# Fill weights of the banded attention: each load but the first placed behind the mask additions of the block whose scores were made last

## The chip, the cores and the metric

The kernel runs on one core of a Trainium2 chip. The metric is the device time of one execution, in microseconds (us). Three runs of the kernel before gave 1305.97, 1306.15 and 1306.93 us; the median is 1306.15 us. A core has a matrix engine (PE, whose weight loads are listed apart as PEld), a vector engine (DVE), an activation engine (ACT), a further engine (POOL) and an engine that here only issues transfers (SP). Each engine carries out its own instructions in a fixed order, which is settled when the kernel is built, and waits on semaphores for the others.

## What is computed

One decoder layer on a sequence of 1024 rows of width 1024: a token mixer, cross-attention, a gated MLP with a short convolution, and a final norm. The change touches the token mixer only. It projects the normalised input once and splits the result over two head groups, a gated linear attention (GLA) and a sliding-window softmax attention in banded blocks of 128 queries. Cut to what matters:

```python
hn = rms_norm(h, norm_mix[l])
proj = hn @ w_in[l]
gq, gk, gv, gr, ga, sq, sk, sv = jnp.split(proj, split_at, axis=-1)
o_gla = gla_mixer(gq, gk, gv, gr, ga, w_alpha[l], b_alpha[l], gla_gain[l])
o_swa = swa_mixer(sq, sk, sv, rel_bias, sinks[l])
h = h + jnp.concatenate([o_gla, o_swa], axis=-1) @ w_out[l]

def swa_mixer(q, k, v, rel_bias, sinks):          # per block of 128 queries, 256 keys
    s = jnp.einsum('bnqhgd,bnkhd->bnhgqk', qb, kk)
    s = jnp.where(mask, s + bias, -jnp.inf)
    m = jnp.maximum(jnp.max(s, axis=-1, keepdims=True), sink)
    p = jnp.exp(s - m)
    p = p / (jnp.sum(p, axis=-1, keepdims=True) + jnp.exp(sink - m))
    o = jnp.einsum('bnhgqk,bnkhd->bnqhgd', p, vv)
```

## The kernel before

Products of 32-bit numbers are made of three products of parts: every operand is split into a high part (ACT, a cast, L110) and a low part (DVE, the difference, L111), and `mm3` (L149, L150, L151) multiplies high by high, high by low and low by high. So the first two products of a weight tile need only its high part, the third its low part.

A weight tile of 1024 by 128 of `w_in` is made ready in four steps, all in `load`: a transfer of 512 KB into one of three staging tiles `st` (`fetch`, issued by SP), a multiplication by the norm's gains in place (DVE, L123), the cast into the high part `w` (ACT, L110), and the difference into the low part `w` (DVE, L111). There are six `w` tiles, that is three pairs.

The stage that the change touches is the banded attention, `swa`. It works on eight blocks, b = 0 to 7. Ahead of the loop the scores of block 0 are made. Then in pass b

1. `swa_softmax(b + 1)`: sixteen score products on PE (L1008) into four banks `psS`, then on DVE eight mask additions with a row maximum (L1017, each two instructions: the addition and the reading of the maximum), small operations on the row factors (`nm`, `es`, `den`), eight exponentials on ACT (L1026), and eight multiplications by the row factors on DVE (L1034); pass 7 has no such step, since there is no block 8;
2. the first half of a column tile of the GLA projection, 24 products on PE into a bank `psF` (`next(fill)`), evicted by DVE at L609;
3. `swa_transposed(b)`: transposes of block b's probabilities on PE, copied by ACT;
4. the second half of the same column tile, 24 products;
5. `swa_values(b)`: the products with the values on PE (L1061), whose result is split (ACT L110, DVE L111 into `pts`) and stored.

PE's order is written out by hand over this loop. It is the code's order. The GLA column tiles are the filling: eight of them, `gk` twice, `gq` twice, `gr` four times, made by the generator in `cols_gla`, one in each pass. Pass b uses column tile b. In pass 3 the fill also has transposes of the decayed keys (L711) ahead of its products, with copies on ACT (L712).

The orders of DVE, ACT and SP are not written out by hand here: when the kernel is built, a scheduler places their instructions. Nothing kept it from placing the preparation of the fill weights well ahead of their use. The call `issue_after(x)`, used elsewhere in the kernel already, tells it that the instructions made in its block that run on the same engine as x must stand behind x in that engine's order.

Of the kernel before, what the change touches and what calls it, by code (L numbers as in the profile page):

```python
# [24 lines left out]
ALU = mybir.AluOpType  # L25
# [3 lines left out]
P = 128  # L29
# [3 lines left out]
NK = D // P  # L33
# [10 lines left out]
NEG = -1e30  # L44
# [17 lines left out]
class Layer:  # L62
# [550 lines left out]
    def cols_gla(self, keep):  # L613


        w = self.a["w_in"][0]
        self.gk, self.gq, self.gr = [], [], []
        first = [self.load_cols(w, 256, self.mix_gains(0, NK))]

        def parts():  # L620
            for tiles, tag, c0, n, scale in ((self.gk, "gk", 256, 2, 1.0), (self.gq, "gq", 0, 2, 0.125),
                                             (self.gr, "gr", 1024, 4, 1.0)):
                for t in range(n):
                    dst = keep(tag, bufs=n)
                    tiles.append(dst)
                    weights = first.pop() if first else self.load_cols(w, c0 + P * t, self.mix_gains(0, NK))
                    yield from self.cols_parts(dst, weights, scale)
        return parts()

# [367 lines left out]
    def swa_softmax(self, b, new):  # L997

        nc = self.nc
        q = slice(b * P, (b + 1) * P)  # L1000
        k0, nk = self.swa_keys(b)
        off = 256 - nk
        ps = [[self.bank("S").rearrange("p (t k) -> p t k", t=2) for _ in range(2)] for _ in range(2)]
        for u in range(2):
            for t in range(2):
                for g in range(2):
                    pr = slice(64 * g, 64 * g + 64)
                    nc.tensor.matmul(ps[u][g][:, t, :nk], lhsT=self.sq[2 * u + t][pr, q], rhs=self.sk[pr, k0:k0 + nk],  # L1008
                                     start=True, stop=True)
        probs = []  # L1010
        for u in range(2):
            prob = new("prob", [P, 4, 256], bufs=4)
            mx = self.small("mx", [P, 4])
            for g in range(2):
                for t in range(2):
                    n = 2 * g + t
                    nc.vector.tensor_tensor_reduce(out=prob[:, n, :nk], in0=ps[u][g][:, t, :nk],  # L1017
                                                   in1=self.bias[g][:, 2 * u + t, off:], scale=1.0, scalar=NEG,
                                                   op0=ALU.add, op1=ALU.max, accum_out=mx[:, n:n + 1])
            nm = self.small("nm", [P, 4])  # L1020
            us = slice(4 * u, 4 * u + 4)
            nc.vector.scalar_tensor_tensor(out=nm, in0=mx, scalar=-1.0, in1=self.nsink[:, us], op0=ALU.mult,
                                           op1=ALU.min)
            den = self.small("den", [P, 4])
            for n in range(4):
                last = nc.scalar.activation(out=prob[:, n, :nk], in_=prob[:, n, :nk], func=AF.Exp,  # L1026
                                            bias=nm[:, n:n + 1], accum_out=den[:, n:n + 1])
            es = self.small("es", [P, 4])
            nc.vector.tensor_tensor(out=es, in0=nm, in1=self.sink[:, us], op=ALU.add)
            last = nc.scalar.activation(out=es, in_=es, func=AF.Exp)  # L1030
            nc.vector.tensor_tensor(out=den, in0=den, in1=es, op=ALU.add)
            nc.vector.reciprocal(out=den, in_=den)
            for n in range(4):
                nc.vector.tensor_scalar(out=prob[:, n, :nk], in0=prob[:, n, :nk], scalar1=den[:, n:n + 1],  # L1034
                                        scalar2=None, op0=ALU.mult)
            probs.append(prob)
        return probs, last
# [977 lines left out]
```

## Time and profile before

| what | us |
|---|---|
| median of three runs | 1306.15 |
| the profiled execution, its own time | 1307.37 |
| its span | 1305.5 |
| PE busy, 0 to 100 us | 94.42 |
| PE busy, 100 to 220 us | 119.42 |
| DVE busy, 100 to 220 us | 86.67 |
| ACT busy, 100 to 220 us | 64.47 |
| PE busy, 220 to 600 us | 379.82 |
| PE busy, 600 us to the end | 697.74 |

The span is what the trace covers; the execution's own time has 1.9 us more around it. The stretch from 100 to 220 us holds nearly the whole loop over the blocks. Rows of the timeline give the start and the length in us, then engine, line, operation, what it writes and reads, and in brackets the idle time ahead of it with what ended it. Products of PE overlap: the spacing of their starts is their price, not their length.

### The profile page before, as it was taken

Reading aid. Unit: us, or ns where it says so; the run is one execution under the profiler, and the core shown is the slowest. Engines: PE = TensorE matmul, PEld = TensorE weight load, DVE = VectorE, ACT = ScalarE, POOL = GpSimd, SP = SyncE. Lnnn points to the kernel's source line nnn. Section 1 sums busy time; section 2 is a strip of 40 time slices with the busy share of each in tenths; the row PEclk is TensorE's granted clock in tenths of the full one; section 3 lists DMA queues with packets and bytes.
Section 4 is the critical chain, followed back from the end, with each engine's and each line's share of the span. In section 5 each row is a group of like instructions: output and inputs, shape, how many; then the busy total and the mean of one; then the engine's idle time right before and its main releaser. Section 6 shows DMA issues by size and latency. Waiting matters only on the chain.

```text
span 1305.5 us, 17288 instructions
## 1 busy us (share of the span) xinstructions
PE 1291.4 (99%) x6539; PEld 1073.8 (82%) x6539; DVE 948.3 (73%) x1630; ACT 610.0 (47%) x1087; POOL 99.1 (8%) x173
## 2 busy tenths in 40 slices
PE   8999999999999999999999999999999999999997
PEld 8887777989888888888888888888888888888886
DVE  6848764368544333599689988888888886999687
ACT  5525545346433333565556544443444444454455
POOL 1400111101122000001100000000000000000001
PEclk9999999999999999999999999999999999999999
DMA  7642211239844311106422342232223138710204
GB/s 223 186 117 65 62 57 61 65 124 296 224 148 158 117 56 59 33 33 202 122 65 81 113 130 98 80 97 86 76 81 97 66 109 318 282 65 9 73 17 153
DMA packets 140056, 146.89 MB, mean 113 GB/s; under 512 B 15825, under 2 KB 108166, under 8 KB 139974
## 3 DMA queue, kind: packets, MB, share of 16 engines
q1 hardware_dynamic: 127670, 106.82, 26.6%
q0 software_dynamic: 12144, 38.71, 8.4%
q8 instruction: 51, 0.84, 0.3%
q10 hardware_dynamic: 160, 0.27, 0.1%
q14 instruction: 31, 0.25, 0.1%
HBM read 109.06 MB, written 38.28 MB: 113 GB/s over the span
## 4 chain that ended last, share of the span: by engine, by line
PE 96%; DVE 2%; DMA 1%; ACT 0%; issue 0%; SPq 0%; DVEq 0%; ACTq 0%
PE psS L1592 15%; PE psF L1592 13%; PE psF L149 10%; PE psF L150 10%; PE psF L151 10%; PE psS L1707 5%; PE psF L1707 5%; PE psS L1369 3%; PE psS L149 2%; PE psS L151 2%; PE psS L150 2%; PE psO L1707 2%; PE psT L1707 2%; PE psO L149 2%; PE psO L150 2%; PE psO L151 2%
## 5 line engine op out<-in xcount | busy, mean ns | idle before, releaser
L110 ACT CAST w<-st 128x1024 fp32r<-128x1024 f32 (+1 forms) x144 | 124.4, 866 | 251.9 <-PE psF L150 70.9
L111 DVE TENSOR_TENSOR w<-st,w 128x1024 fp32r<-128x1024 f32 (+1 forms) x144 | 142.4, 991 | 76.3 <-ACT w L110 75.6
L1621 DVE SCALAR_TENSOR_TENSOR uy<-uy,vec,uy 128x1023 f32<-128x1023 f32 (+1 forms) x88 | 112.1, 1279 | 1.9 <-ACT uy L1619 1.5
L1707 PE MATMUL psF<-w,w 128*128 128x512 f32 x318 | 89.3, 389 | 0.5 <-DVE w L111 0.5
L1707 PE MATMUL psS<-w,w 128*128 128x512 f32 x318 | 89.0, 389 | 0.0
L1592 PE MATMUL psS<-a,w 128*128 128x512 f32 x360 | 86.5, 389 | 0.0
L149 PE MATMUL psF<-xh,w 128*128 128x512 f32 x208 | 83.0, 399 | 0.0
L151 PE MATMUL psF<-xh,w 128*128 128x512 f32 x208 | 81.5, 392 | 0.0
L150 PE MATMUL psF<-xl,w 128*128 128x512 f32 x208 | 81.2, 390 | 0.0
L1592 PEld LDWEIGHTS psS<-a,w 128*128 128x128 f32 x360 | 67.6, 188 | 14.0
L1592 PE MATMUL psF<-a,w 128*128 128x512 f32 x324 | 77.8, 389 | 0.0
L1592 PEld LDWEIGHTS psF<-a,w 128*128 128x128 f32 x324 | 60.8, 188 | 12.6
L1707 PEld LDWEIGHTS psF<-w,w 128*128 128x128 f32 x318 | 59.6, 188 | 13.2 <-DVE w L111 0.9
L1707 PEld LDWEIGHTS psS<-w,w 128*128 128x128 f32 x318 | 59.7, 188 | 12.4
L1619 ACT ACTIVATE uy<-uy,vec 128x1024 f32<-128x1024 f32 x44 | 54.7, 1246 | 18.6 <-DVE uy L1612 18.3
L149 PE MATMUL psF<-act,w 128*128 128x512 f32 x160 | 63.2, 395 | 0.0
L150 PE MATMUL psF<-act,w 128*128 128x512 f32 x160 | 62.8, 392 | 0.0
L151 PE MATMUL psF<-act,w 128*128 128x512 f32 x160 | 62.5, 391 | 0.0
L1592 PE MATMUL psS<-act,wx 128*128 128x512 f32 x240 | 57.7, 389 | 0.0
L1592 PE MATMUL psS<-act,w 128*128 128x512 f32 x240 | 57.7, 389 | 0.0
L1592 PEld LDWEIGHTS psS<-act,wx 128*128 128x128 f32 x240 | 45.0, 188 | 9.4
L1592 PEld LDWEIGHTS psS<-act,w 128*128 128x128 f32 x240 | 45.0, 188 | 9.3
(464 smaller groups left out, 3082.6 us busy)
## 6 DMA issues: line engine op xcount, KB each, us to landing
st<-in_w_up_dram SPq DMA_DIRECT2D x44, 512.0 KB, 4.0
g_d<-uy POOLq DMA_DIRECT2D x22, 512.0 KB, 2.9
act<-in_w_down_dram SPq DMA_DIRECT2D x12, 512.0 KB, 9.1
st<-g_d SPq DMA_DIRECT2D x10, 512.0 KB, 3.9
res<-g_d SPq DMA_DIRECT2D x10, 512.0 KB, 9.1
st<-in_w_in_dram SPq DMA_DIRECT2D x9, 512.0 KB, 6.6
xt_d<-pts POOLq DMA_DIRECT2D x16, 256.0 KB, 4.6
ow_d<-pts POOLq DMA_DIRECT2D x32, 128.0 KB, 3.2
```

The source lines that it names most:

```text
L110: h = nc.scalar.copy(out=hi, in_=src)
L111: l = nc.vector.tensor_tensor(out=lo, in0=src, in1=hi.bitcast(F32), op=ALU.subtract)
L149: mm(out, lhsT=lh, rhs=rh, start=start, stop=False)
L150: mm(out, lhsT=lh, rhs=rl, start=False, stop=False)
L151: mm(out, lhsT=ll, rhs=rh, start=False, stop=stop)
L1369: mm(ps, lhsT=left[n][l][:, q], rhs=right[n][q][r], start=new and q == 0 and i == 0, stop=new and q == 3 and i == 2, skip_group_check=not new)
L1592: nc.tensor.matmul(ps, lhsT=b[l][:, q], rhs=a[q][r], start=first and q == 0 and n == 0, stop=first and q == 3 and n == 2, skip_group_check ...
L1619: nc.scalar.activation(out=y, in_=u, func=AF.Identity, scale=self.v("cw2", j), bias=self.v("conv_b", j))
L1621: nc.vector.scalar_tensor_tensor(out=y[:, s:], in0=u[:, :T - s], scalar=self.v(nm, j), in1=y[:, s:], op0=ALU.mult, op1=ALU.add)
L1707: nc.tensor.matmul(ps[i], lhsT=g[:, l, tk], rhs=w[:, r], start=first and k == 0 and m == 0, stop=first and k == n - 1 and m == 2, skip_gro ...
```

## The change

The last mask addition of each block is kept as `self.masked`, and the load of each fill weight but the first runs within `issue_after` of it.

```diff
                 for t in range(n):
                     dst = keep(tag, bufs=n)
                     tiles.append(dst)
-                    weights = first.pop() if first else self.load_cols(w, c0 + P * t, self.mix_gains(0, NK))
+                    with self.tc.issue_after(self.masked.ins):
+                        weights = first.pop() if first else self.load_cols(w, c0 + P * t, self.mix_gains(0, NK))
                     yield from self.cols_parts(dst, weights, scale)
...
             for g in range(2):
                 for t in range(2):
                     n = 2 * g + t
-                    nc.vector.tensor_tensor_reduce(out=prob[:, n, :nk], in0=ps[u][g][:, t, :nk],
-                                                   in1=self.bias[g][:, 2 * u + t, off:], scale=1.0, scalar=NEG,
-                                                   op0=ALU.add, op1=ALU.max, accum_out=mx[:, n:n + 1])
+                    masked = nc.vector.tensor_tensor_reduce(
+                        out=prob[:, n, :nk], in0=ps[u][g][:, t, :nk], in1=self.bias[g][:, 2 * u + t, off:], scale=1.0,
+                        scalar=NEG, op0=ALU.add, op1=ALU.max, accum_out=mx[:, n:n + 1])
+            self.masked = masked
```

Since `swa_softmax(b + 1)` runs ahead of the fill of pass b, `self.masked` is the last mask addition of block b + 1 when the load of column tile b is made, for b = 1 to 6. In pass 7 it is still that of block 7. The load of tile 0 was made earlier and is not tied.

The first place is DVE at the start of the loop and in pass 1. Before, the multiplication by the gains for column tile 1 (`st_1282`) stands among the mask additions of block 0 (`prob_1047`, `prob_1069`; each `ISA` row with a maximum `mx` alone is the reading):

```order
L1017 ISA prob_1069,mx_1070<-psS_1037,bias_593 128x128
L1017 ISA mx_1070 128x1
L123 TENSOR_TENSOR st_1282<-st_1282,vec 128x1024
L1017 ISA prob_1047,mx_1048<-psS_1036,bias_594 128x128
L1017 ISA mx_1048 128x1
```

Now it stands behind the last mask addition of block 2 (`prob_1259` from the bank `psS_1228`), and the low part `w_1286` a few rows further on:

```order
L1018 ISA prob_1259,mx_1260<-psS_1228,bias_594 128x256
L1018 ISA mx_1260 128x1
L123 TENSOR_TENSOR st_1282<-st_1282,vec 128x1024
L1033 TENSOR_TENSOR den_1245<-den_1245,es_1250 128x4
L1024 SCALAR_TENSOR_TENSOR nm_1265<-mx_1260,nsink 128x4
L703 TENSOR_TENSOR gk_1147<-gk_1147,ke_1438 128x1024
L1034 RECIPROCAL den_1245<-den_1245 128x4
L1031 TENSOR_TENSOR es_1272<-nm_1265,sink 128x4
L111 TENSOR_TENSOR w_1286<-st_1282,w_1285 128x1024
```

The row moved two blocks down; five more such pairs moved in the same way, each to behind the mask additions of its pass. On PE nothing moved. In pass 1 its rows are, in both kernels but for line numbers, the last scores of block 2 and then the first products of column tile 1, which read the high part `w_1285` twice and the low part `w_1286` once:

```order
L1009 MATMUL psS_1227<-sk_672,sq_915 128x256
L1009 MATMUL psS_1228<-sk_672,sq_915 128x256
L149 MATMUL psF_1289<-xh_132,w_1285 128x512
L150 MATMUL psF_1289<-xl_133,w_1285 128x512
L151 MATMUL psF_1289<-xh_132,w_1286 128x512
```

So the product that needs `w_1285` stood right behind the scores of block 2 and still does.

The second place is ACT in pass 3, where the exponentials of block 4 (`prob_1562`, `prob_1584`) run and column tile 3 is used (its high part is `w_1622`). Before:

```order
L1026 ACTIVATE prob_1562,den_1570<-prob_1562,nm_1568 128x256 x4
L1030 ACTIVATE es_1575<-es_1575 128x4
L1026 ACTIVATE prob_1584,den_1592<-prob_1584,nm_1590 128x256 x4
L1030 ACTIVATE es_1597<-es_1597 128x4
L712 COPY ke_1438<-psO_1612 128x512
```

Now:

```order
L1028 ACTIVATE prob_1562,den_1570<-prob_1562,nm_1568 128x256 x4
L1032 ACTIVATE es_1575<-es_1575 128x4
L713 COPY ke_1438<-psO_1606 128x512
L713 COPY ke_1438<-psO_1612 128x512
L1028 ACTIVATE prob_1584,den_1592<-prob_1584,nm_1590 128x256 x4
L1032 ACTIVATE es_1597<-es_1597 128x4
L110 CAST w_1622<-st_1619 128x1024
```

The cast of tile 3, which had stood three blocks earlier, now stands behind all eight exponentials of block 4. In passes 1, 2, 4, 5 and 6 the cast stands behind the first four exponentials and ahead of the second four. The third place is DVE in the same pass, behind the mask additions of block 4. Now it reads:

```order
L123 TENSOR_TENSOR st_1619<-st_1619,vec 128x1024
L1033 TENSOR_TENSOR den_1570<-den_1570,es_1575 128x4
L1024 SCALAR_TENSOR_TENSOR nm_1590<-mx_1585,nsink 128x4
L1034 RECIPROCAL den_1570<-den_1570 128x4
L1031 TENSOR_TENSOR es_1597<-nm_1590,sink 128x4
L1036 TENSOR_SCALAR prob_1562<-prob_1562,den_1570 128x256 x4
L1033 TENSOR_TENSOR den_1592<-den_1592,es_1597 128x4
L1034 RECIPROCAL den_1592<-den_1592 128x4
L1036 TENSOR_SCALAR prob_1584<-prob_1584,den_1592 128x256 x4
L111 TENSOR_TENSOR w_1623<-st_1619,w_1622 128x1024
```

There the low part `w_1623` stands behind all eight multiplications by the row factors; in passes 2, 4 and 5 it stands behind the first four, in pass 1 behind a multiplication of the keys (L703) and in pass 6 behind the gains of tile 7. The orders of POOL and SP are the same in both kernels.

## The prediction

> **What bounds the kernel now.** The page's first lines say which engine to follow, and the waits of PE say whether anything holds it up.
>
> ```profile
> span 1305.5 us, 17288 instructions
> ...
> PE 1291.4 (99%) x6539; PEld 1073.8 (82%) x6539; DVE 948.3 (73%) x1630; ACT 610.0 (47%) x1087; POOL 99.1 (8%) x173
> ```
>
> ```profile
> PE psO L260 <- DMA vrows<-in_norm_mix_dram: 3.2, 1, 3.2
> PE psF L149 <- ACT w L113: 1.2, 1, 1.2
> PE psS L521 <- DMA gr<-in_x_dram: 1.2, 1, 1.2
> PE psF L1707 <- DVE w L111: 0.5, 1, 0.5
> PE psS L1008 <- DVE mx L1017: 0.4, 1, 0.4
> ```
>
> PE is idle for 1305.5 - 1291.4 = 14.1 us in all. The five waits (total, times, longest) sum to 6.5 us; the first three are the start, and the only one in the banded attention is 0.4 us, for a score bank that DVE had not read yet. So a microsecond for which PE is made to wait there is a microsecond of the span: later there is 0.5 us of waiting to absorb it. What DVE and ACT do counts only where PE ends up waiting.
>
> Next, the timeline of one pass, that in which block 6 gets its scores (b = 5), on PE, then on DVE, then on ACT.
>
> ```profile
> 185.19 1.94 PE L1061 MATMUL psO<-pts,sv 128*64 128x512 f32 x8
> 187.06 2.00 PE L1008 MATMUL psS<-sk,sq 64*128 64x256 f32 x16
> 188.98 0.50 PE L149 MATMUL psF<-xh,w 128*128 128x512 f32 x1
> 189.32 0.39 PE L150 MATMUL psF<-xl,w 128*128 128x512 f32 x1
> 189.55 0.40 PE L151 MATMUL psF<-xh,w 128*128 128x512 f32 x1
> ```
>
> ```profile
> 185.29 0.69 DVE L609 SCALAR_TENSOR_TENSOR gr<-psF,rbx 128x512 f32<-128x512 f32 x1 [4.44 <-PE psF L151]
> 186.15 1.23 DVE L111 TENSOR_TENSOR w<-st,w 128x1024 fp32r<-128x1024 f32 x1 [0.16 <-ACT w L110]
> 187.82 0.69 DVE L111 TENSOR_TENSOR pts<-psO,pts 128x512 fp32r<-128x512 f32 x1 [0.44 <-ACT pts L110]
> 188.43 0.41 DVE L1017 CUSTOM_DVE_ANT_0 prob<-psS,bias 128x256 f32<-128x256 f32 x1
> ...
> 191.44 0.08 DVE L1017 DVE_READ_ACCUMULATOR2_ANT mx<- 128x1 f32 x1
> ```
>
> ```profile
> 190.12 0.51 ACT L1026 ACTIVATE prob<-prob,nm 128x256 f32<-128x256 f32 x1 [2.33 <-DVE nm L1022]
> ...
> 192.10 0.19 ACT L1030 ACTIVATE es<-es 128x4 f32<-128x4 f32 x1
> ```
>
> Call the start of the scores V (187.06). PE is through with them at V+1.9 and goes on at once with the column tile, at V+1.9, V+2.3 and V+2.5 (the third product, the first that reads the low part). DVE is only at V+1.4 with its first mask addition and at V+4.4 through with the eight: it had to wait for the values of the block before (`pts`, at V+0.8). PE could go on since the column tile's weights had long been made; DVE's 186.15 row is the low part of a tile for a later pass. That lead is what the change takes away.
>
> **What the change costs, part by part.** It adds and removes no work. It moves seven preparations of weights, each of three instructions, whose durations are, with the multiplications that now stand ahead of some low parts (groups between 100 and 215 us):
>
> ```profile
> L111 DVE TENSOR_TENSOR w<-st,w 128x1024 fp32r<-128x1024 f32 x7 | 8.5, 1214 | 0.2 <-ACT w L110 0.2
> L123 DVE TENSOR_TENSOR st<-st,vec 128x1024 f32<-128x1024 f32 x7 | 8.4, 1213 | 0.0
> L110 ACT CAST w<-st 128x1024 fp32r<-128x1024 f32 x7 | 7.3, 1047 | 43.9 <-PE psS L1008 23.8 <-PE psF L150 16.7 <-DVE st L123 3.4
> L1034 DVE TENSOR_SCALAR prob<-prob,den 128x256 f32<-128x256 f32 x56 | 16.0, 348 | 0.3
> ```
>
> In pass 5 the chain that PE waits for is now: mask additions done at V+4.4; gains 1.21, to V+5.6; cast 1.05 and about 0.1 of handing over, to V+6.7 (ACT is free by then: its first four exponentials ran from V+3.1 to V+5.0). So PE's first product of the tile goes from V+1.9 to V+6.7. The low part does not follow the cast at once: on DVE four small operations (some 0.4) and four multiplications of block 6 (four by about 0.28, since they overlap: 1.1) stand between, so it starts at V+7.1 and ends 1.21 later, at V+8.3. PE's third product waits for that: V+8.3 instead of V+2.5, **5.8 us late**. The rest of the pass finds its operands ready: the transposes of block 5 need probabilities made a pass earlier, and the second half of the tile the same weights.
>
> Pass 4 reads the same: 5.8. In passes 1 and 6 a multiplication of 1.2 stands where the four of 1.1 stood; 5.9 each. In pass 2 the queue ahead of the mask additions is longer:
>
> ```profile
> 135.28 2.00 PE L1008 MATMUL psS<-sk,sq 64*128 64x256 f32 x16
> 136.53 0.68 DVE L111 TENSOR_TENSOR pts<-psO,pts 128x512 fp32r<-128x512 f32 x1
> ```
>
> `pts` starts at V+1.25 instead of V+0.76. Two key multiplications ran ahead of it then; in the new order they still do, the second in the place of a low part of the same length. That is 0.5 more: 6.3. Pass 3 has the key transposes ahead of the tile, and its cast stands behind two copies and the second four exponentials:
>
> ```profile
> 151.99 2.00 PE L1008 MATMUL psS<-sk,sq 64*128 64x256 f32 x16
> 153.92 1.09 PE L711 MATMUL psO<-ident,gr 128*128 128x128 f32 x8
> ...
> 155.31 0.39 PE L151 MATMUL psF<-xh,w 128*128 128x512 f32 x1
> ```
>
> ```profile
> L712 ACT COPY ke<-psO 128x512 f32<-128x512 f32 x4 | 2.2, 592 | 1.9 <-PE psO L711 1.9
> ```
>
> The first exponentials end at V+5.1, two copies (about 0.5 each, overlapped) at V+6.2, four exponentials (192.10 - 190.12 = 2.0) at V+8.2, the cast at V+9.3. DVE meanwhile waits for the second four, then multiplies them, to V+9.9, and the low part is there at V+11.1. The third product stood at 155.31 - 151.99 = V+3.3; 7.8 late. Pass 7 makes no scores, and its tile is made ready in pass 6 behind tile 6's: nothing.
>
> Sum of the six: 5.8 + 5.8 + 5.9 + 5.9 + 6.3 + 7.8 = **37.5 us**, with perhaps 0.5 of error on each, so 3 in all. On the other side, the gains of tile 1 no longer stand among the mask additions of block 0, so PE's wait of 0.4 there goes: -0.4.
>
> Transfers: the staging tiles of passes 1 to 3 can still be filled ahead of the loop, as only three fit. Each later transfer starts when the tile three loads before it has been split, which is now in the pass before the last of the three; a pass is over 16 us long (151.99 - 135.28 = 16.7), so it is hidden. What comes behind the loop (the row weights) is made in pass 6 and 7 on DVE and ACT, some 20 us ahead of its use: nothing, or a microsecond or two if a transfer lands late.
>
> **The clock.** A gap of this length has no equal within this kernel. PE would be idle from V+1.9 to V+6.7, 4.8 us, in four passes, for 5.2 in pass 2, and in pass 3 from V+2.9 (the end of L711) to V+9.3, 6.4. The two ends of the trace show what such idleness does. At the start, 272-wide products stand 0.22 apart until 12.09 and 0.12 apart from 13.59 on, though nothing else about them changed; at the end, after the last product, the granted clock (the column behind the engines' busy times) falls:
>
> ```profile
> 7.76 0.59 PE L149 MATMUL psF<-w,xh 128*128 128x272 f32 x1 [1.22 <-ACT w L113]
> ...
> 11.87 0.43 PE L150 MATMUL psF<-w,xh 128*128 128x272 f32 x1
> 12.09 0.43 PE L151 MATMUL psF<-w,xl 128*128 128x272 f32 x1
> ...
> 13.59 0.29 PE L151 MATMUL psF<-w,xl 128*128 128x272 f32 x1
> 13.71 0.29 PE L149 MATMUL psF<-w,xh 128*128 128x272 f32 x1
> ```
>
> ```profile
> 1296.70 1.52 PE L1707 MATMUL psS<-pre,pre 128*128 128x512 f32 x6
> ```
>
> ```profile
> 1302.00:1303.00 1.00, 0.00 (x0) 0.00 (x0) 0.00 (x0) 0.00 (x0) 0.00 (x0) 0.92 0.55 207
> 1303.00:1304.00 1.00, 0.00 (x0) 0.00 (x0) 0.00 (x0) 0.00 (x0) 0.00 (x0) 0.50 0.86 318
> ```
>
> A mean of 0.92 over that microsecond is full clock to 1302.84, then half: 4.6 us behind the end of the last product (1298.22). And at the start PE worked steadily from 7.76 to about 12.2, 4.5 us, before it ran at full pace; at 0.12 for 0.22 those 4.5 us hold some 2.5 us of work, so one fall of the clock costs about 2.0. Four gaps of 4.8 and one of 5.2 lie barely above 4.6, with an error of 0.5 on each; one drop does not tell whether 4.6 is a threshold or luck. I take the long gap as certain and two of the other five, three falls, **6 us**; the ends are none (0) and six (12).
>
> [...]
>
> Sum: 37.5 - 0.4 + 6 = 43 us on the profiled execution's own 1307.37, of which 1305.5 is the span. That execution stands 1.2 above the median of 1306.15, so against the median the forecast is **1349 us** (+3.3%).
>
> **Rivals.**
> - *The clock falls in every gap*: 12 instead of 6, 1355, up to 1359 with the error of the waits. For it: every gap is longer than the only one measured. Chance 0.18.
> - *The clock stays*: 1306.15 + 37.1 = 1343. For it: two short products run in each gap, and four gaps are within the error of 4.6. Chance 0.09.
> - *More than the first products come late*: DVE and ACT, an added three microseconds behind in every pass, hold up the transposes or the row weights as well, 1 to 3 us a pass: 1356 to 1365. Against it: their operands are a pass old. Chance 0.05.
> - *Only the high part is waited for*, because the scheduler's order leaves the low part in time: gaps of 4.8 alone, about 6 by 4.8, 1335. Against it: the low part's row stands behind multiplications in all six passes. Chance 0.04.
> - *The other side*: the tie binds a block earlier than its words, so that the gains of tile b stand behind the mask additions of block b, made in the pass before. Then the weights are 8 us or more ahead of PE, the wait of 0.4 goes, and the time is 1305.7, not slower. It decides by one row, whether the gains of `st_1282` follow `psS_1094`, the last bank of block 1, or `psS_1228`, that of block 2. The order shows the latter, and PE's row of tile 1 right behind it. Chance 0.02.
>
> **How the numbers follow.** The forecast, the waits with one to four falls of the clock, 1342 to 1353, has 0.62. About 0.2% (2.6 us) is what a measurement of this kernel can tell from no change. All cases but the last are slower by far more: slower 0.98; the last, at 1305.7, is the same, with a little of it faster: same 0.015, faster 0.005. The range runs from 1338 (no fall, waits 3 us short, and a little) to 1359 (six falls, waits 3 us long).
>
> **What would show it.** PE's waits list L149 waiting for ACT `w` six times, some 4.8 us each and over 6 in pass 3, and L151 waiting for DVE `w` six times for about a microsecond more. PE's busy time stays near 1291 if the clock holds, and the granted clock shows 0.5 behind some of the gaps if not. The first mask addition stays at about V+1.4. The forecast is wrong if PE meets the tile's weights ready (another order than shown), or if DVE reaches the mask additions much sooner than V+1.4 now that it has less ahead of them; pass 5 says not, where `pts` waited for ACT and not for DVE's own queue.

## The result, and the profile after

The changed kernel takes **1353.26 us** (median of three runs, 1352.62 to 1354.29) where the kernel before takes 1306.15 (1305.97 to 1306.93): a ratio of 1.0357, with a 95% interval of 1.0344 to 1.0371. The profiled execution took 1354.29 us, 46.9 more than that of before (1307.37).

The first lines of the page of the changed kernel, beside those of before:

```profile
span 1352.4 us, 17286 instructions
...
PE 1306.8 (97%) x6539; PEld 1082.8 (80%) x6539; DVE 949.6 (70%) x1630; ACT 610.0 (45%) x1087; POOL 99.1 (7%) x173
```

The matmuls are as many as before, 6539, and DVE, ACT and POOL did the same work (DVE 1.3 us more, the other two the same). PE is the one engine whose busy time grew, by 15.4 us, and it is idle for 1352.4 - 1306.8 = 45.6 us instead of 14.1. So the time went two ways: PE waits more, and the same products take longer. The waits of PE (total, times, longest) show the first:

```profile
PE psF L149 <- ACT w L110: 30.5, 6, 6.2
PE psO L260 <- DMA vrows<-in_norm_mix_dram: 3.1, 1, 3.1
PE psF L151 <- DVE w L111: 2.5, 6, 0.6
```

The first and the third row are new, and both come six times: once in each pass from 1 to 6. Pass 5 shows the whole mechanism. Its timeline in the changed kernel (start, duration, engine, line, what; in brackets the wait ahead of it), on PE, DVE and ACT:

```profile
219.22 2.00 PE L1009 MATMUL psS<-sk,sq 64*128 64x256 f32 x16
225.96 0.79 PE L149 MATMUL psF<-xh,w 128*128 128x512 f32 x1 [4.74 <-ACT w L110]
226.55 0.63 PE L150 MATMUL psF<-xl,w 128*128 128x512 f32 x1
227.48 0.80 PE L151 MATMUL psF<-xh,w 128*128 128x512 f32 x1 [0.30 <-DVE w L111]
228.08 0.63 PE L149 MATMUL psF<-xh,w 128*128 128x512 f32 x1
228.50 0.63 PE L150 MATMUL psF<-xl,w 128*128 128x512 f32 x1
```

```profile
219.98 0.69 DVE L111 TENSOR_TENSOR pts<-psO,pts 128x512 fp32r<-128x512 f32 x1 [1.83 <-ACT pts L110]
220.59 0.41 DVE L1018 CUSTOM_DVE_ANT_0 prob<-psS,bias 128x256 f32<-128x256 f32 x1
...
223.26 0.42 DVE L1018 CUSTOM_DVE_ANT_0 prob<-psS,bias 128x256 f32<-128x256 f32 x1
...
223.61 1.22 DVE L123 TENSOR_TENSOR st<-st,vec 128x1024 f32<-128x1024 f32 x1
...
225.15 1.14 DVE L1036 TENSOR_SCALAR prob<-prob,den 128x256 f32<-128x256 f32 x4
226.21 1.22 DVE L111 TENSOR_TENSOR w<-st,w 128x1024 fp32r<-128x1024 f32 x1
```

```profile
224.86 1.04 ACT L110 CAST w<-st 128x1024 fp32r<-128x1024 f32 x1 [0.41 <-DVE st L123]
```

With V = 219.22: the first mask addition is at V+1.4, as before, the last ends at V+4.5, the gains run to V+5.6, the cast to V+6.7, and the first product of the tile starts there (225.96). Four multiplications (225.15) stand ahead of the low part, which runs from V+7.0 to V+8.2, and the third product starts at V+8.26 (227.48) instead of V+2.5.

The last two rows on PE show the second way. Consecutive products stand 0.42 apart (228.08, 228.50), where the prediction's rows of before have them 0.23 apart (189.32, 189.55). The granted clock was 0.50 there (224.97 to 231.79) and 1.00 from 95 to 260 us in the kernel before. In the rows below the columns are stretch, length, the busy time of PE, PEld, DVE, ACT and POOL with their counts, the granted clock of PE (1.00 is full), the share of the DMA engines and GB/s; the stretches are those between which the clock changed, or multiples of 3.41 us from them.

```profile
122.57:125.98 3.41, 1.22 (x2) 0.50 (x2) 3.35 (x8) 3.40 (x13) 0.00 (x0) 0.50 0.12 38
143.05:146.46 3.41, 0.84 (x8) 0.40 (x6) 3.41 (x19) 0.62 (x3) 2.73 (x4) 1.00 0.38 115
146.46:149.87 3.41, 0.76 (x2) 0.50 (x2) 3.35 (x14) 3.40 (x11) 0.00 (x0) 0.50 0.13 41
149.87:153.29 3.42, 2.97 (x8) 2.05 (x7) 2.34 (x7) 1.26 (x7) 0.00 (x0) 0.50 0.43 121
173.77:177.18 3.41, 1.22 (x2) 0.50 (x2) 2.54 (x7) 1.70 (x6) 0.00 (x0) 0.50 0.00 0
194.25:197.66 3.41, 1.74 (x16) 1.20 (x14) 2.84 (x14) 1.08 (x4) 2.08 (x4) 1.00 0.26 77
197.66:201.07 3.41, 0.31 (x1) 0.30 (x2) 3.41 (x16) 3.00 (x11) 0.68 (x1) 1.00 0.25 77
201.07:204.49 3.42, 2.88 (x7) 1.83 (x6) 2.63 (x8) 1.71 (x9) 0.00 (x0) 0.50 0.31 90
221.55:224.97 3.42, 0.00 (x0) 0.00 (x0) 3.38 (x18) 2.28 (x10) 1.56 (x3) 1.00 0.51 153
224.97:228.38 3.41, 2.12 (x4) 1.30 (x5) 2.79 (x10) 3.01 (x10) 0.00 (x0) 0.50 0.00 0
228.38:231.79 3.41, 3.41 (x9) 2.65 (x9) 2.11 (x6) 0.00 (x0) 0.00 (x0) 0.50 0.40 115
231.79:235.20 3.41, 3.41 (x19) 2.83 (x19) 0.39 (x1) 0.00 (x0) 0.00 (x0) 1.00 0.00 0
248.86:252.28 3.42, 1.48 (x3) 0.76 (x4) 3.42 (x9) 3.01 (x10) 0.00 (x0) 0.50 0.08 25
```

The clock fell in **every one of the six passes**: at 122.57, 146.46, 173.77, 201.07, 224.97 and 248.86, each time for two stretches of 3.41 us (pass 5 is shown whole: half at 224.97, full again at 231.79; nine products in the stretch from 228.38, nineteen in the next). PE was not idle throughout ahead of each of them: in the stretch ahead of 146.46 it was at work for 0.84 of 3.41 us, in that ahead of 201.07 for 0.31.

The account of the 46.9 us. The third product came late by 5.95, 6.4, 7.7, 5.8, 5.8 and 5.7 us in passes 1 to 6, each read as for pass 5: **37.35**. (The first two products of each tile run within it and count as busy, so it isn't the same split as that of idle and busy time above.) Behind the third product, the half clock still lasted 3.34, 2.51, 3.29, 5.62, 4.32 and 3.67 us (from its start to the end of the fall; pass 5: 231.79 - 227.48), 22.75 in all; a product that takes 0.43 there instead of 0.23 loses 0.47 of that time: **10.6**, or 1.8 a fall. And from the scores of block 0 to those of block 2 the changed kernel is **1.1** faster, which e1 and e5 below take apart. Together 37.35 + 10.6 - 1.1 = 46.9.

### The profile page after: what moved, and what is told of

The parts are those of the page before. It is cut to its first block, busy times and chain, and to the rows that moved or that the text cites. A ratio compares the mean times of both kernels' runs of the same rounds, so it can differ in the third digit from the quotient of the medians.

```text
span 1352.4 us, 17286 instructions
## 1 busy us (share of the span) xinstructions
PE 1306.8 (97%) x6539; PEld 1082.8 (80%) x6539; DVE 949.6 (70%) x1630; ACT 610.0 (45%) x1087; POOL 99.1 (7%) x173
## 4 chain that ended last, share of the span: by engine, by line
PE 94%; DVE 3%; ACT 1%; issue 0%; DMA 0%; SPq 0%; ACTq 0%; DVEq 0%
PE psS L1594 14%; PE psF L1594 13%; PE psF L151 10%; PE psF L149 9%; PE psF L150 9%; PE psS L1709 6%; PE psF L1709 6%; PE psS L1371 3%; PE psS L149 2%; PE psS L151 2%; PE psS L150 2%; PE psO L1709 2%; PE psT L1709 2%; PE psO L149 2%; PE psO L150 2%; PE psO L151 2%
## 5 line engine op out<-in xcount | busy, mean ns | idle before, releaser
L110 ACT CAST w<-st 128x1024 fp32r<-128x1024 f32 (+1 forms) x144 | 124.3, 866 | 210.9 <-PE psF L150 48.7
L111 DVE TENSOR_TENSOR w<-st,w 128x1024 fp32r<-128x1024 f32 (+1 forms) x144 | 142.4, 991 | 76.8 <-ACT w L110 76.6
L149 PE MATMUL psF<-xh,w 128*128 128x512 f32 x208 | 88.7, 426 | 30.5 <-ACT w L110 30.5
L151 PE MATMUL psF<-xh,w 128*128 128x512 f32 x208 | 87.1, 419 | 2.5 <-DVE w L111 2.5
L150 PE MATMUL psF<-xl,w 128*128 128x512 f32 x208 | 86.1, 414 | 0.0
L149 PEld LDWEIGHTS psF<-xh,w 128*128 128x128 f32 x208 | 42.5, 204 | 42.5 <-ACT w L110 32.7
L151 PE MATMUL psF<-act,w 128*128 128x512 f32 x160 | 62.5, 391 | 0.0
L151 PEld LDWEIGHTS psF<-xh,w 128*128 128x128 f32 x208 | 41.8, 201 | 15.8 <-DVE w L111 6.8
```

Source lines behind the costliest of these rows:

```text
L110: h = nc.scalar.copy(out=hi, in_=src)
L111: l = nc.vector.tensor_tensor(out=lo, in0=src, in1=hi.bitcast(F32), op=ALU.subtract)
L149: mm(out, lhsT=lh, rhs=rh, start=start, stop=False)
L150: mm(out, lhsT=lh, rhs=rl, start=False, stop=False)
L151: mm(out, lhsT=ll, rhs=rh, start=False, stop=stop)
```

## The experiments

In what follows *the tie* is the `issue_after` of the change, and *a fall* a time at half clock. The theory: the time is the wait for the weights that now follow the mask additions (some 36 us net), and on top a lower clock for PE, which the idle gaps bring about. Its rivals: the clock has no part in it, and the rest is something that the changed order does to DVE and ACT; or the clock falls only over a wholly idle stretch. The edits are to the changed kernel. Each run is compared with runs of the kernel before on the same chip: 1306.5 for e1 to e4, 1306.42 for e5 and e6.

### e1: tied, but made a pass ahead

```diff
+            plan = [(tiles, tag, c0, n, scale, t) for ... for t in range(n)]
+            weights = first.pop()
+            for i, (tiles, tag, c0, n, scale, t) in enumerate(plan):
...
+                if i < 7:
                     with self.tc.issue_after(self.masked.ins):
-                        weights = first.pop() if first else self.load_cols(w, c0 + P * t, self.mix_gains(0, NK))
-                    yield from self.cols_parts(dst, weights, scale)
+                        following = self.load_cols(w, plan[i + 1][2] + P * plan[i + 1][5], self.mix_gains(0, NK))
+                yield from self.cols_parts(dst, weights, scale)
+                weights = following
```

> The tie stays, behind the mask additions of the block scored last, but each load is written one pass ahead of its use: the tile tied in pass b is that of pass b + 1. Theory (the cost is PE waiting for a chain that starts only behind the mask additions): PE's waits for w go, the granted clock stays 1.00, and the time is that of the kernel before, 1305 to 1307 us. Rival (the tie itself costs, by the work that it pushes between the small operations of the softmax on DVE and ACT): these stand at the same places as in the changed kernel, so most of the 47 us stays, above 1330 us.

Measured: 1305.28 us (11 runs, 1304.65 to 1305.88), ratio 0.999 (0.9982 to 0.9999). The tie is the same and stands in the same place, but what is tied is the tile of the next pass. PE's waits for `w` of L110 and L111 are gone from the list, the tiles' products take at most 0.50 us each through the banded attention (0.63 to 0.80 at half clock in the changed kernel), and the granted clock of the whole span is 0.998 (0.983 in the changed kernel). So the tie as such costs nothing: the loss is the tile's being needed in the very pass whose mask additions it follows. The version even stands 1.2 us below the kernel before, at the edge of what can be told. On PE, from the scores of block 0 to those of block 2:

```profile
99.70 1.16 PE L1013 MATMUL psS<-sk,sq 64*128 64x128 f32 x16
101.02 2.49 PE L1013 MATMUL psS<-sk,sq 64*128 64x256 f32 x16 [0.15 <-DVE mx L1022]
...
116.47 2.00 PE L1013 MATMUL psS<-sk,sq 64*128 64x256 f32 x16
118.40 0.50 PE L149 MATMUL psF<-xh,w 128*128 128x512 f32 x1
```

That is 16.77 us (99.70 to 116.47), and the tile's first product follows the scores at V+1.9, without a wait.

### e5: made a pass ahead, without the tie

The edit against e1:

```diff
                 if i < 7:
-                    with self.tc.issue_after(self.masked.ins):
-                        following = self.load_cols(...)
+                    following = self.load_cols(...)
```

> As the kernel whose loads are written a pass ahead, but without the tie. There the scores of blocks 0 and 1 took 1.1 us less on PE than in the kernel before. If that gain is the tie's (the gains of tile 1 no longer stand among the mask additions of block 0, so the score banks come free sooner), it goes here: 1306 to 1307 us, with the gains of tile 1 among the mask additions again. If the gain is that of writing the load earlier, it stays: 1305 to 1305.5 us.

Measured: 1306.84 us (11 runs, 1305.85 to 1308.01), ratio 1.0001 (0.9992 to 1.001). The same stretch on PE:

```profile
99.99 2.88 PE L1012 MATMUL psS<-sk,sq 64*128 64x128 f32 x24
103.30 1.62 PE L1012 MATMUL psS<-sk,sq 64*128 64x256 f32 x8 [0.43 <-DVE mx L1021]
...
117.87 2.00 PE L1012 MATMUL psS<-sk,sq 64*128 64x256 f32 x16
```

It is 17.88 us again, as in the kernel before, with the same wait of 0.43. So the 1.1 us come from the tie, which keeps a multiplication of 1.2 us out of the mask additions of block 0, and not from the load's being made earlier. Why 1.1 and not 0.43 shows in the waits of the weight loads between 99 and 120 us, first of the kernel before, then of the changed one:

```profile
PEld psS L1008 <- DVE mx L1017: 1.5, 4, 0.8
```

```profile
PEld psS L1009 <- DVE mx L1018: 0.5, 2, 0.3
```

The score banks were waited for four times, 1.5 us, and now twice, 0.5. The row of the matmuls showed 0.43 us of that.

### e2: PE kept at work through the wait

Eighteen products whose result isn't used stand ahead of the tile in passes 1 to 6; 18 by 0.23 is 4.1 us of a gap of some 4.8.

```diff
-    def cols_parts(self, t, w, scale):
+    def cols_parts(self, t, w, scale, extra=0):
...
+            for _ in range(extra if h == 0 else 0):
+                xh, _ = self.xact(0, 0)
+                self.nc.tensor.matmul(ps, lhsT=xh[:, 0:P], rhs=xh, start=True, stop=True)
...
-                    yield from self.cols_parts(dst, weights, scale)
+                    yield from self.cols_parts(dst, weights, scale, 18 if 1 < count < 8 else 0)
```

> The changed kernel, with 18 products of no use (4.1 us at full clock, on data long there, into the bank that the tile's own products then start afresh) ahead of the tile in the six passes. Theory (of the 47 us some 37 are lateness of the third product and some 10 are work at half clock behind it): the lateness stays and the clock does not fall, 1341 to 1344 us. Rival (the clock costs nothing, since the work behind the wait has slack): 1353 us. If the added products themselves push the tile back: above 1353 us.

Measured: 1345.88 us (four runs, 1342.61 to 1347.75), ratio 1.0303 (1.0286 to 1.0319): **more work in the same gap, and 7 us less time**. Pass 5 on PE:

```profile
212.77 2.00 PE L1014 MATMUL psS<-sk,sq 64*128 64x256 f32 x16
214.69 4.37 PE L608 MATMUL psF<-xh 128*128 128x512 f32 x18
219.51 0.50 PE L149 MATMUL psF<-xh,w 128*128 128x512 f32 x1 [0.44 <-ACT w L110]
...
221.02 0.50 PE L151 MATMUL psF<-xh,w 128*128 128x512 f32 x1 [0.78 <-DVE w L111]
```

The third product is at V+8.25, just where it is in the changed kernel, so the waits are the same; the products behind it take 0.50 instead of 0.80. That settles the first rival: what goes here is the clock's part alone. The profiled execution (1344.51) has one fall left, in pass 3, where the 18 products leave 2.13 us of the gap unfilled:

```profile
171.02:174.43 3.41, 1.79 (x7) 1.19 (x8) 2.28 (x5) 0.51 (x1) 0.00 (x0) 1.00 0.01 2
174.43:177.85 3.42, 3.42 (x10) 2.65 (x9) 0.00 (x0) 0.00 (x0) 0.00 (x0) 0.50 0.53 152
```

With it the account is 37.35 - 1.1 + 3.42 x 0.47 = 37.9 over 1306.5, 1344.4; measured 1344.51. The lowest run, 1342.61, agrees with the account without a fall (1342.75). The median stands 2 us above what the theory gave (1341 to 1344). The granted clock over the whole span, on record for each run, was 0.999 in the lowest run, 0.997 in the profiled one and 0.996 in the two near 1347.5: so the clock was down for longer in these two, but in which passes is not shown.

### e3: only the low part tied

The gains and the cast come as early as before; only the difference that makes the low part stands behind the mask additions.

```diff
+    def load_low_tied(self, pieces, gains):
...
+        self.nc.vector.tensor_tensor(out=st, in0=st, in1=gains.unsqueeze(2)..., op=ALU.mult)
...
+        with self.tc.issue_after(self.masked.ins):
+            self.split(st, hi, lo)
...
-                    with self.tc.issue_after(self.masked.ins):
-                        weights = first.pop() if first else self.load_cols(w, c0 + P * t, ...)
+                    weights = first.pop() if first else self.load_low_tied(self.columns(w, c0 + P * t), ...)
```

> Only the low part is tied; gains and cast run ahead as in the kernel before. Theory of the chain: PE's first two products of a tile come at once, and the third waits for the mask additions and one difference: late by 3.2, 3.5, 2.3, 3.1, 3.1 and 3.1 us, 18 in all, with idle gaps of 2.3 to 3.5 us. If the clock falls only after a stretch of 3.4 us or more without any product, no fall or one: 1323 to 1326 us. If it falls whenever a window of that length is mostly idle (in the changed kernel it fell 2.6 and 2.9 us behind the last product), two to five falls by 1.7: 1327 to 1333 us. Rival to the chain (the high part alone is what costs): 1306 us.

Measured: 1332.83 us (four runs, 1330.96 to 1336.23), ratio 1.0206 (1.019 to 1.0221). The wait came much as foreseen, and it is short, 2.2 to 3.5 us a pass; the third products are late by 3.2, 3.65, 2.3, 3.2, 3.2 and 3.2 us, 18.8 in all where 18.3 was expected:

```profile
PE psF L160 <- DVE w L111: 17.8, 6, 3.5
```

Yet the clock fell in five of six passes. Passes 5 and 4 side by side, each a gap of 3.0 us (pass 5 from 207.85, the end of the second product, to 210.85; pass 4 from 187.84 to 190.87):

```profile
206.30:209.71 3.41, 1.55 (x12) 0.74 (x8) 3.38 (x20) 1.47 (x6) 2.76 (x4) 1.00 0.39 115
209.71:213.13 3.42, 2.28 (x5) 1.82 (x6) 2.55 (x9) 3.42 (x13) 0.00 (x0) 0.50 0.47 134
```

```profile
185.82:189.23 3.41, 2.02 (x16) 1.16 (x12) 3.23 (x16) 1.08 (x5) 2.46 (x4) 1.00 0.34 102
189.23:192.65 3.42, 1.78 (x8) 1.49 (x9) 3.05 (x13) 3.42 (x13) 0.30 (x1) 1.00 0.34 91
```

In pass 5 the gap falls mostly into one stretch of 3.41, of which PE was at work for 1.55 (45%), and the next stretch runs at half. In pass 4 the gap lies over two stretches (189.23 is between them); 2.02 of 3.41 (59%) and 1.78 of 3.42 (52%) were work, and the clock stayed at 1.00. That ends the second rival: the clock fell behind gaps of 2.17 (pass 3) to 3.48 us (pass 2), and PE was at work for 0.41 to 1.55 us of the stretch ahead of each fall. The five falls left 22.1 us at half clock behind the third products, 10.4 by the same 0.47; with the 18.8 of lateness 29.2, where the profiled execution (1336.23) stands 29.7 above before. The four runs spread over 5.3 us, and their granted clocks go with their times: 0.994 at 1330.96, 0.993 at 1331.10, 0.991 at 1334.57 and 0.989 at 1336.23.

### e4: the tie in pass 3 alone

```diff
-                    with self.tc.issue_after(self.masked.ins):
+                    with self.tc.issue_after(self.masked.ins) if c0 == 0 and t == 1 else nullcontext():
```

> Only the tile of pass 3, the dearest, is tied. Theory (each pass costs on its own): one wait of about 6.2 us for the high part, the third product 7.7 late, one fall of the clock, 1.7: 1306 + 9.4, 1314 to 1317 us. Rival (the passes add up on each other, and a single one is made good by the slack of the next): 1306 to 1310 us.

Measured: 1315.75 us (four runs, 1314.78 to 1316.62), ratio 1.0072 (1.0058 to 1.0086), so 9.25 us for the one pass.

```profile
160.84 0.79 PE L149 MATMUL psF<-xh,w 128*128 128x512 f32 x1 [6.22 <-ACT w L110]
...
162.62 0.80 PE L151 MATMUL psF<-xh,w 128*128 128x512 f32 x1 [0.57 <-DVE w L111]
```

The waits are those of the changed kernel's pass 3 (6.22, and 0.56 there), and one fall left 3.39 us at half behind the third product: 7.7 + 3.39 x 0.47 = 9.3. The passes add up one by one; none hands its loss on to the next.

### e6: tied to the fourth mask addition

```diff
-            self.masked = masked
+            if u == 0:
+                self.masked = masked
```

The load then follows the first four of a block's eight mask additions.

> The changed kernel with the tie at the fourth of the eight mask additions. In passes 1 and 2 the order of DVE is that of the changed kernel; in pass 3 the gains come sooner, but the cast still stands behind all exponentials; in passes 4 to 6 gains and cast come 1.5 us sooner and the difference right behind the eighth mask addition. Theory of the chain: third products late by 5.9, 6.4, 7.4, 4.3, 4.3 and 4.3 us, 32.6 in all. If the clock is halved whenever a window of 3.4 us is busy for less than half, it falls in all six passes still, by about 1.6 each: 1306 + 32.6 - 1.1 + 9.6, about 1347, 1344 to 1349 us. If only a wholly idle window counts, passes 4 to 6 (gaps of 3.2) keep the clock: 1341 to 1343 us. If the wait has nothing to do with how far down the tie stands: 1353 us.

Measured: 1349.09 us (four runs, 1348.22 to 1350.4), ratio 1.0323 (1.0307 to 1.0339): 4 us better than the changed kernel, and just above what was expected (1344 to 1349).

```profile
PE psF L149 <- ACT w L110: 26.1, 6, 6.7
...
PE psF L151 <- DVE w L111: 2.7, 5, 0.8
```

Passes 4 to 6 wait 3.1 us instead of 4.75; passes 1 and 2 wait as long as before (4.82 and 5.22), pass 3 longer (6.75). These three gain nothing since the order of the other instructions holds the tile back there, as was expected before the run. In passes 1 and 2 the gains still stand behind the eighth mask addition, where the scheduler put them (in pass 1 the addition starts at 121.94, the gains at 122.28). In pass 3 the gains come early (169.26, ahead of the fifth), but the cast (175.19) still stands behind all eight exponentials, and now behind a copy as well. The third products are late by 5.9, 6.4, 7.8, 4.2, 4.2 and 4.2 us, 32.7 in all where 32.6 was expected. The waits are 28.8 instead of 33.0, and that difference of 4.2 is nearly the whole gain: all six falls remain, those behind gaps of 3.1 us too. The expectation's "less than half" was the author's estimate; no run shows that this share is what decides.

## Why the prediction was right, point by point

- *What bounds the kernel*: shown. DVE and ACT were as busy as before, and each wait of PE's came out at the end.
- *The waits, 37.5 us*: shown, 37.35. Each pass came within 0.2 of its own number (5.9, 6.3, 7.8, 5.8, 5.8, 5.9 against 5.95, 6.4, 7.7, 5.8, 5.8, 5.7), pass 3 with its copies and exponentials and pass 2 with its later `pts` included. e4 measured one of them alone.
- *L151 waiting for a further microsecond*: the sum is right, the row is not. It lists 2.5 us in six, not about 6, because at half clock the first two products themselves took longer (in pass 5 the second started 0.59 behind the first, 0.34 before) and so filled that time; in e2, where the clock mostly held, it is 5.2.
- *The first mask addition at V+1.4*: shown (220.59 - 219.22 = 1.37).
- *The wait of 0.4 that goes*: mis-sized. It was 1.1, as e1 and e5 show. The prediction read the row of the matmuls; the weight loads had waited more often.
- *The clock: "the long gap as certain and two of the other five, three falls, 6 us"*: this is the term that was mis-sized. There were six falls, 10.6 us. What happened is the rival *the clock falls in every gap*, and the time, 1353.26, lies between the forecast's own range (up to 1353) and that rival's 1355. The step that failed is the one from a single drop, behind the last product of the trace, to the number of falls: the prediction took it that a gap of 4.8 us may be too short for one. The three are the author's estimate, and no run shows them. That drop came 4.6 us behind the last product, and no work followed, so it could not show what a gap between two stretches of work does. Here PE had 0.31 to 0.84 us of work in four of the six stretches of 3.41 us ahead of the changed kernel's falls and none in the other two (170.36, 221.55); ahead of e3's falls it had up to 1.55.
- *The price of a fall, 2.0*: near (1.8), but partly by luck. It was taken from 4.5 us of slow products at the start of the kernel (the granted clock is recorded as 1.00 there, and that the clock made them slow was not shown); here a fall lasted 6.83 us, of which 3.8 on average lay behind the third product. That the time is inside the range says nothing for the three falls either, since the range was drawn to hold six.
- *More than the first products late*: not seen; the transposes and the second half of the tile show no wait.
- *Only the high part waited for*, and *the tie a block earlier*: neither happened; the rows of pass 5 show the gains behind the last mask addition of block 6 and the low part behind the multiplications.

On the profiled executions the forecast's sum was 43.1 and came out at 46.9: 4.6 more from the clock, 0.7 less from the gain in block 0, 0.15 less from the waits.

## What to carry to other kernels

Where an engine is hardly ever idle (PE was busy for 99% of the span here), what it needs in a stage should be made in the stage before: the same tie on the load of the next tile cost nothing (e1), and on the load of the current one 47 us. In this kernel the gaps on PE cost more than their length, since products behind them ran at a granted clock of 0.50: 1.8 us more on average for gaps of 4.7 to 6.2, and 2.1 for each fall of e3, whose gaps were 2.2 to 3.5. Such a cost must be added to a sum of waits. And when a row of the matmuls shows a small wait, the rows of the weight loads should be read too.

## What the runs showed of the hardware

What follows is read from the profiled executions of the changed kernel, e2, e3, e4 and e6, in stretches of 3.41 us between about 92 and 263 us.

- The granted clock read 1.00 or 0.50, and within one execution its changes stood at multiples of 3.41 us from one another. A fall lasted 3.41 us (the one of e2, three of e3, one of e6) or 6.83 (all six of the changed kernel, two of e3, the one of e4, five of e6).
- Of stretches ahead of falls, PE was at work for 0% (221.55), 9% (197.66) and 25% (143.05) in the changed kernel, for 45% in e3 (206.30) and for 52% in e2 (171.02). The clock stayed at 1.00 behind one of 51% in the changed kernel (194.25) and one of 52% in e3 (189.23). The busy times are modelled at their ends, and what the clock goes by was not shown.
- There were six falls for six gaps of 4.7 to 6.2 us (changed kernel), six for six of 3.1 to 6.75 (e6), five for six of 2.2 to 3.5 (e3) and one for one of 6.2 (e4).
- In the changed kernel the stretches at half clock from 201.07 (2.88 of 3.42, 84%) and 224.97 (62%) were followed by another at half clock, and those from 149.87 (87%) and 228.38 (100%) by full clock.
